# Expert stage: each next weight part is queued behind the instructions that take the same product's result out of PSUM

## The chip, the cores and the metric

The kernel runs on one core of one Trainium2 chip. The metric is the device time of one execution in microseconds (us). A change of less than 0.5% counts here as no change.

## What is computed (reference, cut)

Two layers of a network on 1024 tokens of width 1024, in float32. The first block and the mixer, attention and cross-attention of the second are not touched by the change. What is touched is the last step, a mixture of 32 experts: every token goes to 2 of them, and their weighted results are added to the token's row.

```python
def hierarchical_moe(h, w_group, b_group, w_router, b_router, w_gate_up, w_down):
    ...                                   # two experts e per token, with weights
    def expert_block(args):
        xb, e = args
        gu = xb @ w_gate_up[e]            # 1024 -> 2 x 512
        return (jax.nn.silu(gu[:, :EXPERT_FF]) * gu[:, EXPERT_FF:]) @ w_down[e]   # 512 -> 1024
    ...
    out = jnp.zeros((n + 1, d), ys.dtype).at[buf_tok].add(ys * buf_w[:, None].astype(ys.dtype))
```

## The kernel before, in words

The kernel is one program of which the expert stage (`moe`) is the last part. Up to 96 tokens of an expert are one block; the loop runs over 32 experts.

**Weights.** An expert has 6 MB of weights. They come by SP's queue in transfers of 1 MB into tiles `raw` (line 2187), of which there are 15 (`NRA`, `NRB`, `NRX`, `NRP` = 6, 6, 1, 2); a transfer into a tile is issued when the tile's last reader is done. Each `raw` holds two *parts*. `parts` makes two tiles of a part: ACT copies it into `wh`, rounded (line 154, called through `act` in `split`), and DVE writes what is left over, `raw - wh`, into `wl` (line 166). There are `NP` = 4 buffers of each. So the split of a part waits for its `raw`, for the product of four parts before to have been finished by PE (it frees the buffer), and DVE's half for ACT's.

**Products.** A part feeds one *product*: six matmuls of 512 columns on PE (lines 173 to 175, `mm3`), which add into a PSUM tile. `work` lists the products in order. In the turn of expert e there are eight `up` products of e, namely four into `pg` of c = 0 (the gate) and four into `pg` of c = 1, and then four `down` products of expert e - 1, two into `pd` of c = 0 and two into `pd` of c = 1. Twelve products and six transfers make a turn. `pg` has three PSUM buffers, `pd` two, and `pt` (for transposes) three.

**What takes results out of PSUM.** These instructions run on ACT and DVE too, between the splits:

- `gated` after the last product of a `pg`: for c = 0 a tanh on ACT into `tg` and a product on DVE; for c = 1 a product on DVE.
- `scaled` after the last product of a `pd`: ACT writes half of `y` (line 154). It frees the `pd` buffer. After both halves POOL issues the scatter of `y` (line 2290).
- `x_split` after the sixth product of a turn: PE has transposed the next expert's tokens (line 2232) into `pt`, and ACT and DVE write `xh` and `xl`, in two pieces each.
- `a_split` after the second product of a turn: PE has transposed `tg` of the expert before (line 2263), and ACT and DVE write `ah` and `al`, the left-hand side of its `down` products.

**Order.** Each engine runs its instructions in a fixed order, which a scheduler writes when the program is built. It works with priorities and with estimated times; `tc.issue_after(i)` adds an edge without a semaphore: what is traced under it and runs on the engine of i stands behind i in that engine's order. In the main loop, the results' readers of product n have an edge to the split of part n + 3. The call `ahead(n + NP)`, which traces the split of part n + 4, has none. That split and the readers of product n become possible at the same moment, when PE is through with product n.

Of the kernel before, what the change touches and what calls it, by code (L numbers as in the profile page):

```python
# [16 lines left out]
AF = mybir.ActivationFunctionType  # L17
OP = mybir.AluOpType
# [13 lines left out]
NP = 4  # L32
# [97 lines left out]
class Model:  # L130
# [2077 lines left out]
    def moe(self):  # L2208
        nc, A, tc = self.nc, self.A, self.tc
        with self.pool("moe") as T, self.pool("mg", bufs=3, space=PSUM) as PG, \  # L2210
# [3 lines left out]
            def gather(u):  # L2214
                return nc.gpsimd.indirect_dma_start(
                    out=u["xt"], out_offset=None, in_=self.x3d,
                    in_offset=bass.IndirectOffsetOnAxis(ap=u["row"], axis=0),
                    bounds_check=1023, oob_is_err=False)

            def parts(raw, h):  # L2220

                hi = self.PARTS.tile([128, 2, 512], F32R, name="wh", tag="wh", bufs=NP)
                lo = self.PARTS.tile([128, 2, 512], F32R, name="wl", tag="wl", bufs=NP)
                return (hi, lo, *self.split(hi, lo, raw[:, 2 * h:2 * h + 2]))

            def x_turn(u):
                u["px"] = []
                for q in range(2):
                    pt = PT.tile([128, 4, BLK], F32, name="pt", tag="pt")
                    for a in range(4):  # L2230
                        k = 4 * q + a
                        nc.tensor.transpose(pt[:, a], u["xt"][:, k * 128:(k + 1) * 128], self.ident[0:BLK, 0:BLK])
                    u["px"].append(pt)

            def x_split(u):
                u["xh"] = T.tile([128, 8, BLK], F32R, name="xh", tag="xh", bufs=2)
                u["xl"] = T.tile([128, 8, BLK], F32R, name="xl", tag="xl", bufs=2)
                for q in range(2):
                    self.split(u["xh"][:, 4 * q:4 * q + 4], u["xl"][:, 4 * q:4 * q + 4], u["px"][q])

            def up(u, c, k2, ws):

# [8 lines left out]
            def gated(u, c):  # L2251

                if c == 0:
                    u["t"] = T.tile([BLK, 512], F32, name="tg", tag="tg", bufs=2)
                    self.act(u["t"], u["pg", 0], AF.Tanh, scale=u["half"])
                    self.stt(u["t"], u["t"], 1.0, u["pg", 0], OP.add, OP.mult)
                else:
                    self.tt(u["t"], u["t"], u["pg", 1], OP.mult)

            def a_turn(u):  # L2260
                u["pa"] = PT.tile([128, 4, BLK], F32, name="pt", tag="pt")
                for a in range(4):
                    nc.tensor.transpose(u["pa"][:, a], u["t"][:, a * 128:(a + 1) * 128], self.ident[0:BLK, 0:BLK])

            def a_split(u):
                if u is U[31]:

                    a = T.tile([128, 2, 4, BLK], F32R, name="ahl", tag="xh", bufs=2)
                    u["ah"], u["al"] = a[:, 0], a[:, 1]
                else:  # L2270
                    u["ah"] = T.tile([128, 4, BLK], F32R, name="ah", tag="ah", bufs=1)
                    u["al"] = T.tile([128, 4, BLK], F32R, name="al", tag="al", bufs=1)
                self.split(u["ah"], u["al"], u["pa"])

            def down(u, c, k2, ws):
                if k2 == 0:
# [7 lines left out]
            def scaled(u, c):  # L2284
                if c == 0:
                    u["y"] = T.tile([BLK, 1024], F32, name="y", tag="y", bufs=NY)
                self.act(u["y"][:, c * 512:c * 512 + 512], u["pd", c], AF.Copy, scale=u["gate"])

            def scatter(u):
                return nc.gpsimd.indirect_dma_start(  # L2290
                    out=self.out, out_offset=bass.IndirectOffsetOnAxis(ap=u["row"], axis=0),
                    in_=u["y"], in_offset=None, bounds_check=1023, oob_is_err=False, compute_op=OP.add)

            U = [{"row": self.lsti[:, e:e + 1], "gate": self.lst[:, 1, e:e + 1], "half": self.lst[:, 2, e:e + 1],
                  "xt": xg[e % 3]} for e in range(32)]
# [3 lines left out]
            def beyond():  # L2299


                ov = T.tile([NOV, 5, 32], F32, name="ov", tag="y", bufs=NY)
                one = T.tile([NOV, 128], F32, name="one")
                r, d = T.tile([NOV, 6], F32, name="ovr"), T.tile([NOV, 2, NOV], F32, name="ovd")
                cn = self.cnt[0:NOV]
                nc.vector.memset(one, 1.0)
                nc.vector.tensor_copy(out=r[:, 0:2], in_=self.iop)
                self.ts(ov[:, 0], cn, float(BLK), OP.is_gt)
                for b in range(2, NB):
                    self.stt(ov[:, 0], cn, float(BLK * b), ov[:, 0], OP.is_gt, OP.add)  # L2310
                nc.vector.tensor_tensor_scan(out=ov[:, 1], data0=one[:, 0:32], data1=ov[:, 0], initial=0.0,
                                             op0=OP.mult, op1=OP.add)
                self.tt(ov[:, 2], ov[:, 1], ov[:, 0], OP.subtract)
                self.ts(ov[:, 3], ov[:, 2], r[:, 0:1], OP.is_le)
                self.stt(ov[:, 3], ov[:, 1], r[:, 0:1], ov[:, 3], OP.is_gt, OP.mult)
                self.tt(ov[:, 4], self.io32[0:NOV], ov[:, 3], OP.mult)
                nc.vector.tensor_reduce(out=r[:, 2:3], in_=ov[:, 4], op=OP.add, axis=AX.X)
                self.stt(ov[:, 4], ov[:, 2], r[:, 1:2], ov[:, 3], OP.subtract, OP.mult)
                nc.vector.tensor_reduce(out=r[:, 3:4], in_=ov[:, 4], op=OP.add, axis=AX.X)
                self.stt(r[:, 4:5], r[:, 3:4], -32.0 * BLK, r[:, 2:3], OP.mult, OP.add)  # L2320
                self.ts(d[:, 0], self.ident[0:NOV, 0:NOV], r[:, 4:5], OP.mult)
                self.ts(d[:, 1], self.ident[0:NOV, 0:NOV], r[:, 2:3], OP.mult)
                nc.vector.tensor_copy(out=res[:, 1, 0:1], in_=ov[0:1, 1, 31:32])
                return one, d

            def spread(one, d):
                po = PT.tile([128, 2, NOV], F32, name="po", tag="pt")
                nc.tensor.matmul(po, one, d, start=True, stop=True)
                nc.vector.tensor_copy(out=off, in_=po[:, 0])
                nc.vector.tensor_copy(out=res[:, 0], in_=po[0:1, 1])  # L2330
# [14 lines left out]
            def ahead(n):  # L2345
                if n < len(work):
                    if n % 2 == 0:
                        self.moe_ahead()
                        raws.append(self.moe_raw.pop(0))
                    ready.append(parts(raws[-1], n % 2))  # L2350
# [6 lines left out]
            for n, (f, e, c, k) in enumerate(work):  # L2357
                u = U[e]
                m = f(u, c, k, ready[n][0:2])
                last = ready[min(n + NP, len(work)) - 1]  # L2360
                with tc.issue_after(m.ins):
                    if f is up and (c, k) == (0, 1) and e > 0:
                        a_turn(U[e - 1])
                    if f is up and (c, k) == (1, 1) and e < 31:
                        x_turn(U[e + 1])
                with tc.issue_after(last[2].ins), tc.issue_after(last[3].ins):
                    if f is up and (c, k) == (0, 1) and e > 0:
                        a_split(U[e - 1])
                    if f is up and k == 3:
                        gated(u, c)  # L2370
                    if f is up and (c, k) == (1, 1) and e < 31:
                        x_split(U[e + 1])
                    if f is down and k == 1:
                        scaled(u, c)
                if f is up and (e, c, k) == (31, 1, 3):
                    a_turn(u)
                    a_split(u)
                ahead(n + NP)
                if f is up and (c, k) == (1, 1) and e < 28:
                    with tc.issue_after(put.ins) if e > 1 else nullcontext():  # L2380
                        gather(U[e + 4])
                if f is down and (c, k) == (1, 1):
                    put = scatter(u)
                    if e == OVAT - 1:
                        over = beyond()
                    if e == OVAT + 2:
                        spread(*over)
# [5 lines left out]
            with tc.For_i(0, n_over, 1) as it:  # L2393
# [15 lines left out]
                u = {"row": row, "gate": lst[:, 1:2], "half": lst[:, 2:3], "xt": xg[0]}  # L2409
# [144 lines left out]
```

## Time and profile before

| what | value |
|---|---|
| three runs | 2479.79, 2487.82, 2490.89 us (median 2487.82) |
| the profiled execution | 2485.62 us, of which the span from first to last instruction is 2483.9 us |
| granted TensorE clock, mean over the span | 0.983 |
| PE (matmuls) | 2355.6 us busy, 95% of the span |
| DVE | 1748.2 us, 70% |
| ACT | 1314.5 us, 53% |
| POOL | 341.5 us, 14% |
| DMA, mean over the span | 159 GB/s |

Busy shares are means over stages of unlike kinds. The expert stage takes the last 590 us or so of the span, from 1883 us on. There the DMA engines move some 370 GB/s, and DVE and ACT are far busier than the means above. The ends of matmuls in the trace are modelled, so PE looks busy up to the next matmul even where it is not at its peak; distances between starts are the safer measure.

### The profile page before, as it was taken

To read this page: it belongs to the slowest core of one execution; us is meant where nothing else is said; L and a number is where in the kernel's file an instruction comes from. 1 tells how busy PE (TensorE), PEld (TensorE's weight loads), DVE (VectorE), ACT (ScalarE), POOL (GpSimd) and SP (SyncE) were. 2 spreads that over 40 slices of the span, in tenths; PEclk is the share of its full clock that TensorE was granted. 3 is DMA by queue.
4 is the path that set the end of the run, shared out by engine and by line. 5 is a ranking of instruction groups with operands and counts; after the bars stand their busy time and mean duration, and the time that the engine had idled before them with its cause. 6 is when DMAs were issued, how large, how long until landed. Compare 5 with 4: busy or idle time off the path is not lost. (4 is left out here: it accounts for less than half of the span.)

```text
span 2483.9 us, 35045 instructions
## 1 busy us (share of the span) xinstructions
PE 2355.6 (95%) x13016; PEld 1936.7 (78%) x13016; DVE 1748.2 (70%) x3344; ACT 1314.5 (53%) x2102; POOL 341.5 (14%) x363
## 2 busy tenths in 40 slices
PE   8999989999999999999899899999997999999998
PEld 6888868787888898798798678887885777666765
DVE  9667767677875666666666744235667999898987
ACT  5344532445645455454445432134435888787886
POOL 1011114100021021121121100000011111111111
PEclk9999999999999999999999999999998999999999
DMA  6322353322221111110111456532267999999992
GB/s 222 99 68 67 117 179 127 123 78 84 72 77 39 64 45 42 51 52 35 56 51 40 144 199 221 176 119 77 85 244 271 368 376 373 371 372 359 368 371 66
DMA packets 103838, 394.32 MB, mean 159 GB/s; under 512 B 14129, under 2 KB 33073, under 8 KB 79089
## 3 DMA queue, kind: packets, MB, share of 16 engines
q1 hardware_dynamic: 85008, 335.18, 37.5%
q0 software_dynamic: 18656, 56.88, 7.3%
q8 instruction: 104, 1.70, 0.3%
q14 instruction: 70, 0.57, 0.1%
HBM read 339.07 MB, written 61.31 MB: 161 GB/s over the span
## 5 line engine op out<-in xcount | busy, mean ns | idle before, releaser
L166 DVE TENSOR_TENSOR wl<-raw,wh 128x1024 fp32r<-128x1024 f32 (+1 forms) x496 | 587.7, 1209 | 130.3 <-ACT wh L154 126.1
L154 ACT ACTIVATE wh<-raw 128x1024 fp32r<-128x1024 f32 (+1 forms) x496 | 512.1, 1048 | 250.0 <-PE pj L174 67.2
L173 PE MATMUL pj<-wh,xnh 128*128 128x256 f32 x768 | 222.2, 289 | 2.1 <-ACT tg L154 1.0
L175 PE MATMUL pj<-wh,xnl 128*128 128x256 f32 x768 | 217.2, 283 | 0.0
L174 PE MATMUL pj<-wl,xnh 128*128 128x256 f32 x768 | 217.0, 283 | 0.0
L175 PE MATMUL pg<-wh,xl 128*96 128x512 f32 x512 | 201.3, 393 | 1.6 <-DVE xl L166 1.6
L174 PE MATMUL pg<-wl,xh 128*96 128x512 f32 x512 | 202.6, 396 | 0.0
L173 PE MATMUL pg<-wh,xh 128*96 128x512 f32 x512 | 200.2, 400 | 0.9 <-ACT xh L154 0.9
L173 PEld LDWEIGHTS pj<-wh,xnh 128*128 128x128 f32 x768 | 145.4, 189 | 3.8 <-ACT pc L154 2.5
L174 PEld LDWEIGHTS pj<-wl,xnh 128*128 128x128 f32 x768 | 145.2, 189 | 0.0
L175 PEld LDWEIGHTS pj<-wh,xnl 128*128 128x128 f32 x768 | 145.1, 189 | 0.0
L154 ACT ACTIVATE e<-sc,st,ss 128x1024 f32<-128x1024 f32 (+7 forms) x128 | 105.7, 829 | 54.2 <-DVE st L158 42.4
L178 POOL TENSOR_TENSOR ss<-ss,mhalf 128x4 f32<-128x4 f32 (+1 forms) x68 | 72.7, 1069 | 343.5 <-DVE ss L163 318.4
L173 PE MATMUL pd<-wh,ah 128*96 128x512 f32 x248 | 98.2, 400 | 16.6 <-ACT y L154 16.6
L175 PEld LDWEIGHTS pg<-wh,xl 128*96 128x96 f32 x512 | 83.1, 162 | 38.6 <-DVE xl L166 3.2
L173 PEld LDWEIGHTS pg<-wh,xh 128*96 128x96 f32 x512 | 83.0, 162 | 33.8 <-ACT xh L154 1.3
L174 PEld LDWEIGHTS pg<-wl,xh 128*96 128x96 f32 x512 | 82.8, 162 | 32.4
L173 PE MATMUL pg<-xnh,wh 128*128 128x512 f32 x256 | 104.9, 410 | 0.4 <-ACT kv L154 0.2
L175 PE MATMUL pg<-xnh,wl 128*128 128x512 f32 x256 | 102.6, 401 | 0.0
L173 PE MATMUL pj<-xnh,wh 128*128 128x512 f32 x256 | 102.2, 400 | 0.0
L174 PE MATMUL pg<-xnl,wh 128*128 128x512 f32 x256 | 102.2, 399 | 0.0
L174 PE MATMUL pj<-xnl,wh 128*128 128x512 f32 x256 | 101.2, 396 | 0.0
(998 smaller groups left out, 6327.5 us busy)
## 6 DMA issues: line engine op xcount, KB each, us to landing
raw<-in_w_gu SPq DMA_DIRECT2D x128, 1024.0 KB, 15.3
raw<-in_w_dn SPq DMA_DIRECT2D x64, 1024.0 KB, 15.9
raw<-in_w_out SPq DMA_DIRECT2D x16, 512.0 KB, 4.6
ta<-tg POOLq DMA_DIRECT2D x32, 256.0 KB, 2.5
t<-ta SPq DMA_DIRECT2D x14, 512.0 KB, 3.9
raw<-in_w_ga SPq DMA_DIRECT2D x12, 512.0 KB, 3.7
raw<-in_w_v SPq DMA_DIRECT2D x12, 512.0 KB, 3.5
xraw<-in_xT SPq DMA_DIRECT2D x8, 512.0 KB, 5.8
```

Source lines behind the costliest of these rows:

```text
L154: return self.nc.scalar.activation(out=out, in_=in_, func=func, **kw)
L166: return (eng or self.nc.vector).tensor_tensor(out=out, in0=a, in1=b, op=op)
L173: mm(ps, l[0], r[0], start=start, stop=False)
L174: mm(ps, l[0], r[1], start=False, stop=False)
L175: return mm(ps, l[1], r[0], start=False, stop=stop)
L178: self.nc.gpsimd.tensor_tensor(out=out, in0=in_, in1=self.mhalf[:, :w], op=OP.pow)
```

## The change

The functions that take results out of PSUM now return the instructions they made. The main loop collects them in `out`, and `ahead(n + NP)` is called under an `issue_after` of each. So the ACT half and the DVE half of the split of part n + 4 stand behind those readers of product n that run on the same engine. No instruction is added or taken away, no semaphore and no buffer is changed, and SP's and POOL's queues keep their order, since the edges tie only instructions of one engine.

```diff
@@ x_split
-                for q in range(2):
-                    self.split(u["xh"][:, 4 * q:4 * q + 4], u["xl"][:, 4 * q:4 * q + 4], u["px"][q])
+                return [i for q in range(2)
+                        for i in self.split(u["xh"][:, 4 * q:4 * q + 4], u["xl"][:, 4 * q:4 * q + 4], u["px"][q])]
@@ gated
-                    self.act(u["t"], u["pg", 0], AF.Tanh, scale=u["half"])
-                    self.stt(u["t"], u["t"], 1.0, u["pg", 0], OP.add, OP.mult)
-                else:
-                    self.tt(u["t"], u["t"], u["pg", 1], OP.mult)
+                    return [self.act(u["t"], u["pg", 0], AF.Tanh, scale=u["half"]),
+                            self.stt(u["t"], u["t"], 1.0, u["pg", 0], OP.add, OP.mult)]
+                return [self.tt(u["t"], u["t"], u["pg", 1], OP.mult)]
@@ a_split
-                self.split(u["ah"], u["al"], u["pa"])
+                return self.split(u["ah"], u["al"], u["pa"])
@@ scaled
-                self.act(u["y"][:, c * 512:c * 512 + 512], u["pd", c], AF.Copy, scale=u["gate"])
+                return self.act(u["y"][:, c * 512:c * 512 + 512], u["pd", c], AF.Copy, scale=u["gate"])
@@ main loop
+                out = []
                 with tc.issue_after(last[2].ins), tc.issue_after(last[3].ins):
                     if f is up and (c, k) == (0, 1) and e > 0:
-                        a_split(U[e - 1])
+                        out += a_split(U[e - 1])
                     if f is up and k == 3:
-                        gated(u, c)
+                        out += gated(u, c)
                     if f is up and (c, k) == (1, 1) and e < 31:
-                        x_split(U[e + 1])
+                        out += x_split(U[e + 1])
                     if f is down and k == 1:
-                        scaled(u, c)
+                        out += [scaled(u, c)]
                 ...
-                ahead(n + NP)
+
+                with ExitStack() as es:
+                    for i in out:
+                        es.enter_context(tc.issue_after(i.ins))
+                    ahead(n + NP)
```

What that does to the order is seen on ACT and DVE. Numbers behind a tile's name tell one buffer's use from the next.

ACT, in the second half of the stage, before the change: from the tanh of one expert (`tg`) on, with the two halves of `y` of the expert before.

```order
L154 ACTIVATE tg_20893<-pg_20843,lst_16019 96x512
L154 ACTIVATE wh_20896<-raw_20471 128x1024
L154 ACTIVATE wh_20909<-raw_20502 128x1024
L154 ACTIVATE wh_20935<-raw_20502 128x1024
L154 ACTIVATE wh_20950<-raw_20533 128x1024
L154 ACTIVATE wh_20961<-raw_20533 128x1024
L154 ACTIVATE y_20810<-pd_20791,lst_16019 96x512
L154 ACTIVATE y_20810<-pd_20816,lst_16019 96x512
L154 ACTIVATE wh_20974<-raw_20559 128x1024
```

ACT, the same two halves of `y` and the same tanh after the change.

```order
L154 ACTIVATE wh_20800<-raw_20381 128x1024
L154 ACTIVATE y_20810<-pd_20791,lst_16019 96x512
L154 ACTIVATE wh_20812<-raw_20381 128x1024
L154 ACTIVATE wh_20825<-raw_20422 128x1024
L154 ACTIVATE y_20810<-pd_20816,lst_16019 96x512
L154 ACTIVATE wh_20836<-raw_20422 128x1024
L154 ACTIVATE wh_20852<-raw_20446 128x1024
L154 ACTIVATE ah_20867<-pt_20862 128x384
L154 ACTIVATE wh_20871<-raw_20446 128x1024
L154 ACTIVATE wh_20883<-raw_20471 128x1024
L154 ACTIVATE tg_20893<-pg_20843,lst_16019 96x512
```

Both halves have moved from behind the tanh of the next turn, and behind five splits of that turn, to their own products: eleven splits (from `wh_20812` to `wh_20961`) now stand behind the first half instead of ahead of it. In the first eight full turns `y` stood in these places before the change too.

DVE in one of those first turns, the change against before: the two pieces of `xl` and one split.

```order
 L166 TENSOR_TENSOR wl_18777<-raw_18242,wh_18776 128x1024
 L166 TENSOR_TENSOR wl_18790<-raw_18297,wh_18789 128x1024
-L166 TENSOR_TENSOR wl_18816<-raw_18297,wh_18815 128x1024
 L166 TENSOR_TENSOR xl_18810<-pt_18799,xh_18809 128x384
 L166 TENSOR_TENSOR xl_18810<-pt_18804,xh_18809 128x384
+L166 TENSOR_TENSOR wl_18816<-raw_18297,wh_18815 128x1024
 L166 TENSOR_TENSOR wl_18831<-raw_18426,wh_18830 128x1024
```

One split has changed places with the `xl` pair, and on ACT its `wh` with the `xh` pair. In the same way one split stands behind `ah` and `al` now, where it stood ahead of them. After the change every turn from the second tanh of the stage to the last but one has the same order on ACT: tanh, two splits, two `xh`, four splits, half of `y`, two splits, half of `y`, two splits, `ah`, two splits.

## Rows read from the trace of the kernel before

**Rows 1.** Busy us of each engine (instructions), PEclk, DMA share, GB/s, by stretch.

```profile
1934.52:2075.64 141.12, 141.12 (x673) 100.62 (x672) 133.81 (x159) 121.54 (x145) 26.07 (x17) 1.00 1.02 375
2111.44:2451.89 340.45, 321.40 (x1514) 225.54 (x1513) 303.78 (x307) 277.32 (x326) 46.36 (x34) 1.00 0.95 346
```

**Rows 2.** Timeline of PE: four transposes of `tg`, in four turns (start, us).

```profile
1934.52 0.49 PE L2263 MATMUL pt<-ident,tg 96*128 96x96 f32 x4
...
2075.64 0.49 PE L2263 MATMUL pt<-ident,tg 96*128 96x96 f32 x4
...
2111.44 0.49 PE L2263 MATMUL pt<-ident,tg 96*128 96x96 f32 x4
...
2451.89 0.49 PE L2263 MATMUL pt<-ident,tg 96*128 96x96 f32 x4
```

**Rows 3.** Groups of PE between 2111.6 and 2452 us: the transposes of `tg`.

```profile
L2263 PE MATMUL pt<-ident,tg 96*128 96x96 f32 x74 | 9.2, 245 | 0.0
```

**Rows 4.** Waits, 2111.6 to 2452 us (us in total, times, longest).

```profile
PE pd L173 <- ACT y L154: 16.6, 12, 1.7
...
ACT wh L154 <- DMA raw<-in_w_gu: 0.6, 2, 0.3
```

**Rows 5.** Timeline of ACT and PE at the first of these waits.

```profile
2118.91 1.06 ACT L154 ACTIVATE wh<-raw 128x1024 fp32r<-128x1024 f32 x1 [0.33 <-PE pg L175]
2120.29 1.06 ACT L154 ACTIVATE wh<-raw 128x1024 fp32r<-128x1024 f32 x1 [0.32 <-PE pg L175]
2121.26 1.25 ACT L154 ACTIVATE y<-pd,lst 96x512 f32<-96x512 f32 x2
...
2121.98 0.48 PE L173 MATMUL pd<-wh,ah 128*96 128x512 f32 x1 [1.72 <-ACT y L154]
```

**Rows 6.** Timeline of ACT in an earlier turn, around `y`.

```profile
2088.68 0.69 ACT L154 ACTIVATE y<-pd,lst 96x512 f32<-96x512 f32 x1 [0.55 <-PE pd L175]
2089.27 2.00 ACT L154 ACTIVATE wh<-raw 128x1024 fp32r<-128x1024 f32 x2
2091.45 0.69 ACT L154 ACTIVATE y<-pd,lst 96x512 f32<-96x512 f32 x1 [0.19 <-PE pd L175]
```

**Rows 7.** Waits, 1934.7 to 2075.9 us: DVE for ACT.

```profile
DVE wl L166 <- ACT wh L154: 7.9, 20, 0.6
```

**Rows 8.** Timeline around `x_split` of an early turn: ACT, DVE, then PE.

```profile
2098.88 2.07 ACT L154 ACTIVATE wh<-raw 128x1024 fp32r<-128x1024 f32 x2
2100.85 0.85 ACT L154 ACTIVATE xh<-pt 128x384 fp32r<-128x384 f32 x2
...
2099.00 3.50 DVE L166 TENSOR_TENSOR wl<-raw,wh 128x1024 fp32r<-128x1024 f32 x3 [0.20 <-ACT wh L154]
2102.42 1.01 DVE L166 TENSOR_TENSOR xl<-pt,xh 128x384 fp32r<-128x384 f32 x2
...
2104.74 0.39 PE L174 MATMUL pd<-wl,ah 128*96 128x512 f32 x1
```

**Rows 9.** Timeline around `a_split` of an early turn: ACT, DVE, then PE.

```profile
2111.64 1.06 ACT L154 ACTIVATE wh<-raw 128x1024 fp32r<-128x1024 f32 x1 [0.32 <-PE pg L175]
2112.61 0.47 ACT L154 ACTIVATE ah<-pt 128x384 fp32r<-128x384 f32 x1
...
2112.73 1.23 DVE L166 TENSOR_TENSOR wl<-raw,wh 128x1024 fp32r<-128x1024 f32 x1 [0.16 <-ACT wh L154]
...
2116.17 0.39 PE L174 MATMUL pg<-wl,xh 128*96 128x512 f32 x1
```

**Rows 10.** DMA between 1930 and 2110 us: packets, MB, share.

```profile
q1 hardware_dynamic: 8454, 61.59, 88.9%
```

**Rows 11.** DMA between 2140 and 2410 us.

```profile
q1 hardware_dynamic: 12525, 91.22, 88.7%
```

**Rows 12.** Issues between 1925 and 1940 us: KB each, median us to landing.

```profile
raw<-in_w_gu SPq DMA_DIRECT2D x3, 1024.0 KB, 10.3
```

**Rows 13.** Issues between 2085 and 2100 us.

```profile
raw<-in_w_gu SPq DMA_DIRECT2D x2, 1024.0 KB, 21.4
```

## The prediction

> **What bounds the kernel now.** I read the busy time by stretch first. From 1934 to 2076 us PE is busy for all of 141.12 us, at a granted clock of 1.00; from 2111 to 2452 us it is busy for 321.40 of 340.45 us at the same clock, though the work of a turn is the same [rows 1]. DVE comes close behind (133.81 of 141.12 us), and the DMA engines are fully busy in the early stretch (share 1.02, 375 GB/s). So in the early stretch PE sets the pace, and later something makes PE wait.
>
> How much is lost I read from distances between starts, since matmul ends are modelled. The transposes of `tg` come once a turn. From 1934.52 to 2075.64 us are 8 turns: 141.12 / 8 = 17.64 us a turn [rows 2]. From 2111.44 to 2451.89 us, 340.45 us, the groups of PE hold 74 transposes: two are the end of the first group, whose start is ahead of the window, and 72 are 18 groups of four, so 18 turns [rows 2, 3]. At the early pace 18 turns are 317.52 us. The loss is **22.93 us**.
>
> Then the waits. PE's own wait in that stretch is for `y`, 16.6 us in 12 waits [rows 4]; in the early stretch the busy time leaves no room for one [rows 1]. One wait from near by shows what it is. ACT makes a `wh` at 2118.91 and one at 2120.29 us, each after a wait for PE, and only then both halves of `y`; 0.72 us after they start, PE's first `down` matmul goes, which had waited 1.72 us [rows 5]. So `y` is not long, it is late in ACT's queue: it frees one of two `pd` buffers, and stands behind a split that waits for the product just before the one that needs the buffer. PE must finish that product, ACT see it (0.32 us), split (about 1 us) and write half of `y` (0.7 us): about 2 us in which PE has nothing. In an early turn the halves of `y` stand alone, 2.8 us apart, each soon after its product [rows 6], and nothing waits for them.
>
> **The change, part by part.**
>
> *`y` moved up* (`scaled`). In the order after the change, both halves have the early turns' places in every turn. The 12 waits go. I price this at the whole 22.93 us and not at 16.6: the loss by turns also holds the matmuls that start slowly after a wait, and the short waits for `xh` and `xl` in turns whose order is upset. The lower bound is 16.6 us, the named wait alone [rows 4].
>
> *Two moved pairs.* In all turns, one split now stands behind the `xh`, `xl` pair, and one behind `ah`, `al`. This is new in the early turns too, so the trace shows no such order; I bound it.
>
> - `x_split`: the split ahead of `xh` was the last of ACT's two up to 2100.95 and of DVE's three up to 2102.50 us [rows 8]. Left where it was, `xh` starts at 2100.85 and ends at 2101.70; with the split behind it, `wh` ends by about 2102.7 (1.06 us), and `wl` by 2103.95 (1.22 us). DVE does the `xl` pair (1.01 us) in between, so only the order is changed there. The `wl` is first used by the second matmul of its product, four products on, at 2104.74 [rows 8]. To spare: 0.8 us.
> - `a_split`: `ah` needs the transposes, which start at 2111.44 and take 0.49 us [rows 2]; with ACT's wait for PE (0.3 us) it starts at 2112.2 and ends near 2112.7. The split's `wh` starts there instead of at 2111.64, 1.0 us later, and its `wl` ends at 2112.73 + 1.0 + 1.23 = 2114.96. It is used at 2116.17 [rows 9]. To spare: 1.2 us.
>
> Both are costed at nothing, covered by the three products that PE still has in hand. If the cover is gone, the price is what ACT puts ahead: 0.85 + 0.47 = 1.32 us a turn [rows 8, 9]. Idle time of DVE limits this as well: 141.12 - 133.81 over 8 turns is 0.91 us a turn [rows 1], most of it already waits for `wh`, 7.9 us [rows 7].
>
> *tanh and its product*: already ahead of their split in the early turns; nothing.
>
> *Instructions, buffers, semaphores*: none added. SP's and POOL's queues have the same order, but SP's transfers go out as DVE frees `raw`, so a faster stage asks for weights sooner.
>
> **What is late next: the weights.** A turn at 17.64 us uses six transfers, one every 2.94 us. The hardware queue moved 61.59 MB in 180 us, 342 GB/s [rows 10]: 1.049 MB every 3.06 us; later 91.22 MB in 270 us, 338 GB/s, 3.10 us [rows 11]. So PE at full pace uses weights faster than they come, by 0.12 us a transfer, and lives on what was loaded ahead. Fifteen buffers are 15 x 2.94 = 44.1 us; less 3.6 us between ACT's first read and DVE's last of a tile (2098.88 to 2102.50 [rows 8]), a transfer has 40.5 us from issue to use. At 2085 us it takes 21.4 [rows 13], so 19 us are in reserve. It is used at about 2129, a turn after 2111.44; 17 more turns of six and some five in the last, shorter one make 107 transfers behind it: 107 x 0.12 = 13 us, and 6 us stay. By the landings the reserve melts faster: from 10.3 us at 1930 [rows 12] to 21.4, 11 us over 160 / 2.94 = 54 transfers, 0.20 each, so 107 x 0.20 = 21 us, and the last ten transfers or so are 2 us late. With 338 GB/s in place of 342 as well, 107 x 0.24 = 26 us, 7 us late. I take nothing lost and keep 0 to 7 us. So far ACT waited 0.6 us for weights [rows 4].
>
> The Trainium skill, *DMA: Bandwidth & Descriptors*, section Specifications, speaks against the change here: it puts HBM's share for a core at about 358 GB/s. This trace has 375 [rows 1], so the measurement decides. Were 358 the limit, a transfer would take an estimated 3.06 x 375 / 358 = 3.21 us, the reserve would be short by 107 x 0.27 - 19 = 10 us, and the time 2475 us.
>
> **Sum.** The profiled execution took 2485.62 us (span 2483.9 and 1.7 around it). Less 22.9 it is 2462.7. It lies 2.2 us under the median of the runs, so on the median: 2487.8 - 22.9 = 2464.9, **2465 us**, or 0.92% less.
>
> **Rivals.**
>
> - *The weights become the bound.* For: PE's demand is above the supply, DMA share 1.02. Against: 19 us of reserve, and the gathers end four experts before the end, which leaves the queue more. Gain 22.9 - 7 = 16, so 2472 us; with the lower bound for `y` as well, 16.6 - 7 = 10 and 2478. The page named above has the same mechanism with a lower limit.
> - *The stall only moves* (the change doesn't do what it says for the time): `y` comes early, but the next thing in the upset turns, `xl`, `xh` or `wl`, holds PE as long. For: DVE is busy 95% of an early turn. Against: with the early turns' order all through, those turns show no wait of PE at all. Time 2488 us.
> - *Slower: the two moved pairs outrun their cover.* DVE idles 0.91 us a turn; if the 1.32 us fall on DVE's path whole, each of about 30 turns grows by up to 1.32: +39.6 - 22.9 = +17 us, 2505 us. It decides from 22.9 / 30 = 0.76 us a turn. Against it: 0.8 and 1.2 us to spare above, and three products between a split and its use.
>
> **How the numbers follow.** Forecast 0.73, weights 0.14, stall moves 0.07, slower 0.06. The three runs of before lie up to 8 us under the median and 3 over it, 0.45% from end to end, so about 0.5% (12.4 us) is what can be told from no change. Faster by more than that: under 2475.4 us; the forecast, and most of the weights' case, with something off for the runs' spread: 0.85. Within: the rest of that, and the stall that moves: 0.10. Slower: 0.05. The range goes from 2456 (the fastest run of before, 2479.8, less 22.9, rounded down) to 2478: both lower bounds at once, the weights' 7 us and the 16.6 us, which takes in either alone (2472 and 2471) with the runs' spread. The last two cases are outside.
>
> **What would show it.** Right: in the profile after, the transposes of `tg` come every 17.64 us from about 1934 to the end of the stage; no wait of PE for `y`; PE busy for all of the later stretch; halves of `y` apart on ACT. The group that starts at 2451.89 us [rows 2] comes near 2429. Weights: ACT's waits for `raw` of several us, after 2380 us or so. Slower: PE waiting for `wl` in every turn, and turns over 18.4 us, early ones too. I would be wrong if some instruction that now comes earlier makes DVE wait for ACT more than its 0.9 us a turn.

## The result, and the profile after

| | before | after |
|---|---|---|
| median (lowest to highest), us | 2488.24 (2479.79 to 2490.89), 4 runs | 2463.65 (2462.76 to 2465.11), 4 runs |
| profiled execution (its span), us | 2485.62 (2483.9) | 2462.98 (2460.8) |
| first `pg` matmul to start of the last matmul, us | 1883.38 to 2472.76: 589.38 | 1882.80 to 2450.25: 567.44 |

The ratio is 0.9908, with a 95% interval of 0.9883 to 0.9932: about 0.9% faster, 2463.65 us where 2465 was forecast. The profiled execution is 22.64 us shorter, and 21.94 of that lie in the stage with the experts.

Busy time of the same two stretches after the change, in the columns of [rows 1]; the second reaches over the same 18 turns.

```profile
1934.52:2075.64 141.12, 140.40 (x667) 99.81 (x666) 133.38 (x158) 120.11 (x144) 28.29 (x16) 1.00 1.01 374
2111.86:2429.38 317.52, 317.52 (x1514) 226.46 (x1513) 296.52 (x307) 271.75 (x325) 49.93 (x34) 1.00 1.00 367
```

PE is busy for all of the later stretch, where it was busy for 321.40 of 340.45 us. The two ends of that stretch on PE's timeline, which answer to [rows 2]:

```profile
2111.86 0.49 PE L2262 MATMUL pt<-ident,tg 96*128 96x96 f32 x4
...
2429.38 0.49 PE L2262 MATMUL pt<-ident,tg 96*128 96x96 f32 x4
```

317.52 us for 18 turns are 17.64 us a turn, to the hundredth the pace of the early turns of before. These turns took 340.45 us, so they give 22.93 us. The other sign is in turn 9 of the stage, below: +0.97 us. Together that is 21.96 us, within 0.02 us of the stage's difference.

All waits of PE after the change from 1900 to 2445 us (total, times, longest), where [rows 4] had 16.6 us for `y`:

```profile
PE pg L174 <- DVE wl L166: 0.7, 1, 0.7
PE pd L173 <- ACT ahl L154: 0.2, 1, 0.2
```

ACT at a turn in the part that was slow before, which answers to [rows 5] and reads like [rows 6]:

```profile
2115.39 0.69 ACT L154 ACTIVATE tg<-pg,lst 96x512 f32<-96x512 f32 x1 [0.56 <-PE pg L175]
...
2118.28 0.87 ACT L154 ACTIVATE xh<-pt 128x384 fp32r<-128x384 f32 x2 [0.30 <-PE pt L2232]
...
2124.38 0.69 ACT L154 ACTIVATE y<-pd,lst 96x512 f32<-96x512 f32 x1 [0.55 <-PE pd L175]
2124.96 2.00 ACT L154 ACTIVATE wh<-raw 128x1024 fp32r<-128x1024 f32 x2
2127.15 0.69 ACT L154 ACTIVATE y<-pd,lst 96x512 f32<-96x512 f32 x1 [0.19 <-PE pd L175]
```

The halves of `y` stand apart, 2.8 us from each other, each after a wait of ACT for its own product (0.55 and 0.19 us), and no longer behind the next tanh.

**What is new, and was not foreseen: turn 9.** It takes 18.61 us (17.64 before). PE waits 0.72 us for a `wl`, because DVE has small operations of `beyond()` (a function of the kernel that runs once; tiles `ov`, `ovr`, `ovd`) in one block just ahead of its splits. DVE and PE after the change:

```profile
2053.91 0.17 DVE L166 TENSOR_TENSOR ov<-ov 22x32 f32<-22x32 f32 x1
...
2055.77 0.23 DVE L162 TENSOR_SCALAR ovd<-ident,ovr 22x22 f32<-22x22 f32 x1
2055.91 2.34 DVE L166 TENSOR_TENSOR wl<-raw,wh 128x1024 fp32r<-128x1024 f32 x2
...
2055.83 0.39 PE L175 MATMUL pg<-wh,xl 128*96 128x512 f32 x1
2056.06 0.40 PE L173 MATMUL pg<-wh,xh 128*96 128x512 f32 x1
2057.18 0.48 PE L174 MATMUL pg<-wl,xh 128*96 128x512 f32 x1 [0.72 <-DVE wl L166]
2057.49 0.40 PE L175 MATMUL pg<-wh,xl 128*96 128x512 f32 x1
```

From 2053.91 to 2055.91, 2.0 us, DVE makes no split. Before the change small operations stood between splits (one at 2051.98, the next at 2054.36 us, and two splits between them), and PE did not wait:

```profile
2051.98 0.17 DVE L158 SCALAR_TENSOR_TENSOR ov<-cnt,ov 22x32 f32<-22x32 f32 x1
2052.09 2.34 DVE L166 TENSOR_TENSOR wl<-raw,wh 128x1024 fp32r<-128x1024 f32 x2
2054.36 0.20 DVE L2311 TENSOR_TENSOR_SCAN ov<-one,ov 22x32 f32<-22x32 f32 x1
```

**The weights.** No wait of ACT for `raw` shows from 2111.6 to 2430 us. But transfers take longer from issue to landing. Queue and issues after the change (2140 to 2410 us; then the one transfer issued at 2349.17 us, and the one issued at 2359.03 us; the last number is the median time to landing):

```profile
q1 hardware_dynamic: 12584, 91.64, 88.7%
raw<-in_w_gu SPq DMA_DIRECT2D x58, 1024.0 KB, 25.0
...
raw<-in_w_gu SPq DMA_DIRECT2D x1, 1024.0 KB, 25.9
...
raw<-in_w_dn SPq DMA_DIRECT2D x1, 1024.0 KB, 25.3
```

and before, from 2140 to 2410 us:

```profile
raw<-in_w_gu SPq DMA_DIRECT2D x58, 1024.0 KB, 16.7
```

The queue carries as much as before (91.64 MB in 270 us, [rows 11]: 91.22), yet the median transfer is issued 25.0 instead of 16.7 us ahead of its landing. The reserve, from a transfer's landing to its first reader on ACT, has melted. The first of the tight places is the transfer of 25.9 us, on the timelines of SP's queue and of ACT:

```profile
2349.17 0.33 SPq L2187 DMA_DIRECT2D raw<-in_w_gu  x1
...
2374.69 1.99 ACT L154 ACTIVATE wh<-raw 128x1024 fp32r<-128x1024 f32 x2
```

Issued at 2349.17, it lands 25.9 us later, at 2375.1; the second of the two splits, which begins at about 2375.6, reads it. **0.6 us** of the reserve are left. The tightest comes three transfers later: issued at 2359.03, landed 25.3 us later, at 2384.3, and read at about 2384.6, which leaves 0.3 us. In the same way the reserve is 30.7 us for the tile used at 1962.5 and 20.6 us at 2128.7.

### The profile page after: what moved, and what is told of

The parts are those of the page before. It is cut to its first block, busy times and chain, and to the rows that moved or that the text cites. A ratio compares the mean times of both kernels' runs of the same rounds, so it can differ in the third digit from the quotient of the medians.

```text
span 2460.8 us, 35005 instructions
## 1 busy us (share of the span) xinstructions
PE 2350.5 (96%) x13016; PEld 1934.6 (79%) x13016; DVE 1741.0 (71%) x3344; ACT 1307.3 (53%) x2102; POOL 351.5 (14%) x363
## 5 line engine op out<-in xcount | busy, mean ns | idle before, releaser
L154 ACT ACTIVATE wh<-raw 128x1024 fp32r<-128x1024 f32 (+1 forms) x496 | 503.5, 1044 | 198.1 <-PE pj L174 68.3
L175 PE MATMUL pj<-xnh,wl 128*128 128x512 f32 x256 | 101.3, 396 | 0.0
```

Source lines behind the costliest of these rows:

```text
L154: return self.nc.scalar.activation(out=out, in_=in_, func=func, **kw)
L175: return mm(ps, l[1], r[0], start=False, stop=stop)
```

## Experiments

Each kernel was run beside the kernel before on the same chip, whose median was 2488 to 2491 us throughout; ratios are against that, with 95% intervals. "18 turns" is always the distance that is 317.52 us after the change and 340.45 us before.

**1. Only `y` is tied.** The main loop of the change, where the other three results are no longer collected:

```diff
-                        out += a_split(U[e - 1])
+                        a_split(U[e - 1])
-                        out += gated(u, c)
+                        gated(u, c)
-                        out += x_split(U[e + 1])
+                        x_split(U[e + 1])
                     if f is down and k == 1:
                         out += [scaled(u, c)]
```

> Only the two halves of y are tied: the split of part n + 4 has an edge behind scaled alone; x_split, a_split and gated are left as in the kernel before. The order on ACT is then that of the early turns of before all through (tanh, three splits, two xh, three splits, half of y, two splits, half of y, three splits, ah, split). Theory (the place of y is the whole cause): as fast as the change, 2463.7 us, or up to 1 us faster, since the wait of 0.72 us that the changed kernel has at 2057 us, for a wl, goes. Rival (the moved xh and ah pairs carry part of the gain): between 2468 and 2485 us.

Measured: 2469.27 us (2464.09 to 2472.8), ratio 0.9909 [0.9893, 0.9925]. PE's timeline:

```profile
2121.63 0.49 PE L2262 MATMUL pt<-ident,tg 96*128 96x96 f32 x4
...
2439.15 0.49 PE L2262 MATMUL pt<-ident,tg 96*128 96x96 f32 x4
```

Again 317.52 us. All of the gain is `y`'s. The time is 1.9 us above the change's on the same chip (2467.39 us, experiment 10), and one turn makes most of that: turn 9, with 20.16 instead of 18.61 us, where the expectation had said that its wait would go. ACT's timeline there:

```profile
2064.02 0.68 ACT L154 ACTIVATE y<-pd,lst 96x512 f32<-96x512 f32 x1 [4.01 <-DVE ovr L2318]
```

The first half of `y` waits for an operation of `beyond()` on DVE; in the kernel `ov` takes one of the three buffers of `y`. The `wh` behind it is late by that, and PE waits 1.25 us for it and then 0.78 us for a `wl`.

**2. All but `y` are tied.**

```diff
                     if f is down and k == 1:
-                        out += [scaled(u, c)]
+                        scaled(u, c)
```

> All edges of the change but those of scaled. In the order on ACT the halves of y then stand in the late turns behind the tanh and two splits of the next turn, and on PE the transposes of the next tokens come behind the first down product, while xh stands ahead of the split of the next but one product. Theory (the place of y): y behind two splits costs nothing by itself, since in the turns of before with one to three splits ahead of y PE has no wait; so there is no wait of PE for y. But a split that is tied behind xh must now wait for late transposes; by the early turns' rows PE would miss its wh by some 2 us a turn in about 17 turns, so 2463.7 + 17 x 2 to 3 = 2498 to 2515 us, with waits of PE for wh. Rival (the edges on the pairs carry the gain): 2465 to 2480 us.

Measured: 2514.93 us (2511.35 to 2519.23), ratio 1.0094 [1.0076, 1.0111]: slower than before, at the upper end of what was expected. The waits of PE in the stage:

```profile
PE pd L173 <- ACT wh L154: 29.3, 32, 1.6
```

and ACT's timeline in one turn:

```profile
2185.14 1.24 ACT L154 ACTIVATE y<-pd,lst 96x512 f32<-96x512 f32 x2
2186.28 1.05 ACT L154 ACTIVATE wh<-raw 128x1024 fp32r<-128x1024 f32 x1
2188.10 0.87 ACT L154 ACTIVATE xh<-pt 128x384 fp32r<-128x384 f32 x2 [0.77 <-PE pt L2232]
2188.86 6.03 ACT L154 ACTIVATE wh<-raw 128x1024 fp32r<-128x1024 f32 x6
```

`y` still stands in a pair, ahead of `xh`. PE waits not for it but for the `wh` of the `down` products, which now stand behind `xh`; and `xh` waits for late transposes, 4.5 us behind the start of the tanh (2183.60 us) where it is 2.9 us after the change. The 18 turns take 365.86 us, 48.3 more than after the change, of which 29.3 are this wait of PE. So the other ties give nothing by themselves, and this set of them, without `y`'s, costs.

**3, 4. `y` late in every turn.** Both halves of `y`, and the scatter with them, are put off to the next turn and made to stand there behind the fifth split after the tanh; in the fourth experiment behind the fourth. The splits that follow are tied behind them (`carry`). All other ties of the change stay.

```diff
-                out = []
+                out, carry = carry, []
...
-                    if f is down and k == 1:
+                    if f is down and k == 1 and e > 29:
                         out += [scaled(u, c)]
...
+                if f is up and (c, k) == (1, 3) and e > 1:
+                    with tc.issue_after(ready[-1][2].ins):
+                        carry = [scaled(U[e - 2], 0), scaled(U[e - 2], 1)]
+                    put = scatter(U[e - 2])
```

Experiment 4 has `(c, k) == (1, 2)` in the first of the added lines for `carry`.

> The changed kernel with both halves of y put, by edges on both sides, behind the fifth split after the tanh of the next turn, in 30 turns; the scatter moves with them. Theory (y behind the fifth split makes PE wait for the product before, a split and half of y): each of 30 turns longer by 1.96 us, as the eight such turns of before were, so 2463.7 + 59 = 2522 us, and 30 waits of PE for y of 1.7 us. Rival (those turns were slow for another reason, such as weights that came late or the scheduler's upset order of xh): 2464 to 2480 us.

> The same with the halves of y behind the fourth split, one split earlier. Theory: the turns of before with four splits ahead of y lost 0 (three turns) or had a wait for y of 0.34 us (two turns), so 30 x 0 to 0.5 us: 2464 to 2479 us. Rival (each place that y is later costs alike, so four fifths of 1.96 us a turn): 2463.7 + 30 x 1.57 = 2511 us.

Behind five splits: 2524.6 us (2520.73 to 2528.33), ratio 1.0132 [1.0114, 1.015]; a turn takes 19.6 us. Behind four: 2482.48 us (2479.37 to 2485.28), ratio 0.9968 [0.9954, 0.9982]; 18.2 us a turn. Waits of PE in the stage, of the first:

```profile
PE pd L173 <- ACT y L154: 51.6, 30, 1.7
```

and of the second:

```profile
PE pd L173 <- ACT y L154: 10.2, 30, 0.3
```

One instance of the first, ACT and then PE:

```profile
2149.56 1.06 ACT L154 ACTIVATE wh<-raw 128x1024 fp32r<-128x1024 f32 x1 [0.32 <-PE pg L175]
2150.52 1.24 ACT L154 ACTIVATE y<-pd,lst 96x512 f32<-96x512 f32 x2
2151.24 0.48 PE L173 MATMUL pd<-wh,ah 128*96 128x512 f32 x1 [1.72 <-ACT y L154]
```

This is the stall of [rows 5], 0.32 us, 1.72 us and all, made in 30 turns by `y`'s place alone. Behind five splits `y` costs 1.96 us a turn (19.6 - 17.64), behind four 0.56. So the time does not rise evenly with the place: most of it comes with the fifth split, the one that waits for the product just before `down`. The fourth experiment came out 3.5 us above the range given for it. That range was read from turns of before in which `xh` stands behind `y`; here the two `xh` stand ahead of it, besides the four splits. That this makes the 0.56 us is not shown. (In the kernel before, ten turns have `y` behind five splits: seven took 19.6 us, two 18.94 and one, which also waits for `xh` and `xl`, 21.61.)

**5, 6. Eleven weight buffers for fifteen,** in the kernel after and in the kernel before:

```diff
-NRA, NRB, NRX, NRP = 6, 6, 1, 2
+NRA, NRB, NRX, NRP = 6, 2, 1, 2
```

> The changed kernel with 11 buffers raw in place of 15 (NRB 2 for 6), the same order. In the changed kernel's trace a transfer landed 30.7 us ahead of its first reader at 1962 us and 0.6 us ahead at 2376 us, 140 transfers later: 0.215 us less with each. Four buffers fewer are 4 x 2.94 = 11.8 us less of reserve. Theory (the weights have almost no room left after the change): the reserve is used up some 55 transfers earlier, and from there on every transfer makes the stage 0.2 us later: 10 to 12 us slower than the change, 2474 to 2476 us where the change has 2463.7, with waits of ACT for raw in the last third of the stage. Rival (weights have room to spare, the reserve only looks small because transfers are issued when a buffer is free): no difference, 2464 us.

> The kernel before with 11 buffers raw in place of 15; the order of the late turns stays of the same kind, with 8 turns in which y stands behind five splits. Theory (before the change the waits for y slowed PE enough for the weights to keep some 20 us ahead): 20 - 12 = 8 us stay, so no difference to before, 2486 to 2490 us. Rival (fewer buffers cost time by themselves): about 10 us slower, 2498 us.

With the change: 2476.26 us (2470.66 to 2479.57), ratio 0.9934 [0.9912, 0.9955], at the upper end of what was expected. 18 turns take 326.71 us, 9.2 more; single turns up to 21.18 us, from turn 20 on. ACT's waits in the stage:

```profile
ACT wh L154 <- DMA raw<-in_w_gu: 19.1, 17, 2.9
...
ACT wh L154 <- DMA raw<-in_w_dn: 9.4, 8, 2.2
```

In the kernel before: 2483.25 us (2478.44 to 2488.42), ratio 0.9968 [0.9953, 0.9983], where no difference was expected. The scheduler chose another order in the late turns: 18 turns lose 20.4 instead of 22.9 us, with 14.1 us of waits for `y`. That is 2.5 of the 8 us. Most of the rest goes with the granted TensorE clock: its mean over the span is 0.983 in these ten runs and 0.981 in the seventeen of before beside them, and among those seventeen alone the time falls as it rises, from 2498.4 us at 0.978 to 2480.99 us at 0.985, or some 2 us for each 0.001; by that the difference is worth an estimated 4 to 5 us. In this stage the clock is 1.00, its upper level, in both kernels, so this lies ahead of it; why the clock was higher is open. ACT waits for `raw` for 0.3 us there. So four buffers that the slower kernel doesn't need for its weights are worth 9 us of the change's gain.

**7, 9. A third `pd` buffer,** taken from the `pt` pool: in the kernel of experiment 3, and in the kernel before.

```diff
-                self.pool("md", bufs=2, space=PSUM) as PD, self.pool("mt", bufs=3, space=PSUM) as PT:
+                self.pool("md", bufs=3, space=PSUM) as PD, self.pool("mt", bufs=2, space=PSUM) as PT:
```

> The kernel with both halves of y behind the fifth split in 30 turns (the one expected at 2522 us), with three PSUM buffers for pd and two for pt in place of two and three. Theory (a late y costs because only two pd buffers are there, so that PE's next down product needs the one that y still reads): with a third buffer the first down product has a free one and the second comes two products later, when y is long done; no waits for y, 2464 to 2467 us, as the change. Rival (the place on ACT costs by itself, since y then delays the splits behind it): 2490 to 2522 us.

> The kernel before, without any of the change's edges, with three PSUM buffers for pd and two for pt in place of two and three. The scheduler then writes another order in the late turns: y stands behind up to seven splits, and in several turns xh stands behind it at the end of the turn. Theory (what counts is whether the reader is out of the way before PE needs the buffer or the result; a third buffer moves that point by one product, and the scheduler moves y and xh later still): fewer waits for y, but waits for xh and xl in their place, 2475 to 2492 us. Rival (a third buffer is a cure by itself, as with y behind five splits in every turn): 2464 to 2468 us, as the change.

In the kernel of experiment 3: 2469.51 us (2466.2 to 2471.91), ratio 0.9908 [0.9883, 0.9934]. PE's timeline, and below it all its waits from 1900 to 2460 us:

```profile
2119.13 0.49 PE L2262 MATMUL pt<-ident,tg 96*128 96x96 f32 x4
...
2436.63 0.49 PE L2262 MATMUL pt<-ident,tg 96*128 96x96 f32 x4
```

```profile
PE pd L173 <- ACT ahl L154: 0.4, 1, 0.4
```

`y` is as late as in experiment 3, and costs nothing: 317.50 us. What made it costly is that two buffers leave PE no third to write.

In the kernel before: 2496.48 us (2486.79 to 2501.11), ratio 1.0035 [1.0023, 1.0047], against an expectation of some gain. The same buffers changed the order that the scheduler chose: `y` went behind up to seven splits, and 18 turns took 346.07 us. PE waits there:

```profile
PE pd L173 <- ACT y L154: 9.7, 6, 1.7
PE pg L173 <- ACT xh L154: 5.2, 6, 0.9
PE pg L175 <- DVE xl L166: 4.5, 7, 0.8
```

So a buffer more is a cure only where the order is held; left free, the delay went further and to other tiles.

**8. Two matmuls for three in the experts' products,** on top of the change, to see what bounds next.

```diff
+    def mm2(self, ps, l, r, start, stop):
+        mm = self.nc.tensor.matmul
+        mm(ps, l[0], r[0], start=start, stop=False)
+        return mm(ps, l[0], r[1], start=False, stop=stop)
...
-                    m = self.mm3(u["pg", c], ...
+                    m = self.mm2(u["pg", c], ...
```

> The changed kernel with two of the three matmuls of every piece of a product in the expert stage: the one with xl or al is left out, so PE has a third less to do there; splits and transfers are all made. It measures what stands behind PE now. Theory (weights and DVE are within a few per cent of PE): the weights need some 3.06 us each, 18.4 us a turn once the reserve is gone, and DVE is busy 16.7 of 17.64 us of a turn; so the stage ends with the last transfers and the time is 2450 to 2464 us, though PE has some 160 us less to do. Rival (PE alone bounds the stage): below 2400 us.

One execution, on another chip than the result's: 2459.91 us (span 2457.9). Its busy time from the second tanh's transposes to the last but one, 29 turns:

```profile
1913.85:2424.31 510.46, 418.99 (x1743) 242.71 (x1742) 476.84 (x518) 425.28 (x522) 280.04 (x56) 0.96 1.00 370
```

A third of the products' matmuls is gone, and the mean turn is 510.46 / 29 = 17.60 us. Undisturbed early turns take 16.2 us, and DVE is busy in all of them (81.07 of 81.07 us from 1930.06 to 2011.13 us); later ones take 17 to 20, with ACT waiting for weights:

```profile
ACT wh L154 <- DMA raw<-in_w_gu: 18.8, 15, 2.2
ACT wh L154 <- DMA raw<-in_w_dn: 13.8, 10, 2.4
```

Three turns are much longer. In the turns of 21.85 and 27.54 us ACT waits with the first half of `y`, 6.9 us for an operation of `beyond()` and 13.0 us for a scatter of an earlier `y`: both hold buffers of `y`. In the turn of 25.55 us ACT waits for weights, up to 2.4 us at a time. In all, the 18 late turns take 326.64 us, 9.1 more than after the change, and the turns ahead of them 12.6 less. So with a third less work for PE the span is only 3 us shorter, in one run.

**10. The change once more,** beside the last of these.

> The changed kernel as it is, beside the kernel before on this chip, for the variants above to be compared with: 0.991 of before, 2464 to 2470 us. If the ratio is above 0.9925, the gain of 24.6 us was partly a matter of the first chip.

Measured: 2467.39 us (2466.3 to 2468.82), ratio 0.9919 [0.9904, 0.9934], turn 9 at 18.62 us, the other turns as in the first run of the change. Of the kernels that do all the work none is faster than the change by more than the runs spread.

Here ACT does wait for weights, 2.7 us in five waits, the longest among those for the `down` weights:

```profile
ACT wh L154 <- DMA raw<-in_w_dn: 1.3, 2, 0.9
```

Yet the 18 turns take 317.52 us: a transfer that came up to 0.9 us too late for ACT cost PE nothing there.

## Why the prediction was right

- **The bound and the loss.** PE at 17.64 us a turn was the pace, and 22.93 us were lost in 18 turns. Those turns now take 317.52 us, so the term came out whole. That PE set the pace shows in experiment 8 too: with less work for PE the early turns fall from 17.64 to 16.2 us. The lower bound of 16.6 us was too low by 6.3 us, and both reasons that the prediction gave for taking more are in the trace of before. Its other waits of PE in these turns are 2.5 us:

```profile
PE pg L175 <- DVE xl L166: 1.6, 3, 0.7
PE pg L173 <- ACT xh L154: 0.9, 1, 0.9
```

  The other 3.8 us are 0.24 for each of the 16 waits. Experiment 3 has the same difference (a wait of 1.72 us costs 1.96 a turn), and turn 9 too (0.72 and 0.97). Only part of it is a slow start. In the rows of turn 9 the starts ahead of the wait are 0.23 us apart (2055.83 to 2056.06), but a matmul is modelled as 0.40 us long, so the row counts the wait from 0.17 us too late. The start behind the wait then takes 0.31 us to come (2057.18 to 2057.49), 0.08 more than the 0.23.
- **The mechanism.** A late read of one of two `pd` buffers. Experiment 1 gives the gain by `y` alone, 3 makes the stall in every turn by place alone, and 7 takes it away by a third buffer with the place unchanged. The rival that the stall only moves is out: PE waits 0.9 us in all.
- **The two moved pairs.** Costed at nothing; 18 late turns at 17.64 us in the mean and the early ones at 17.63 to 17.64 say so (one turn between them takes 18.16 us in both kernels). The +0.97 us of turn 9, where the `ov` block takes 2.0 us of DVE and leaves no cover, is not theirs: experiments 2 and 7 tie both pairs, and turn 9 takes 17.64 us there; experiment 1 ties `y` alone, and it takes 20.16. So it comes with `y`'s new place; why the small operations then stand in one block is not shown. The prediction priced turns that looked alike and never looked for work that comes once.
- **The weights.** Nothing was lost, as forecast, but not by the forecast's margin of 6 us, and this part is luck. The reserve at 2128.7 us was 20.6 us (19 predicted). By 2375.6 us, 84 transfers on, 20.0 us were gone, 0.24 a transfer, the highest of the three rates worked out, and not the 0.12 taken. At that rate 107 transfers would have ended 5 us late. What saved it is that the weight queue got faster when the gathers had ended, which the prediction named as an argument and left out of the sum. The last gather is issued at 2365.80 us; from 2340 to 2376 us the weight queue carried 12.31 MB, 342 GB/s, and from 2380 to 2416 us 13.52 MB, 376 GB/s, or 2.79 us a transfer, less than the 2.94 in which PE uses one. The queue of the gathers and scatters went from 0.98 to 0.53 MB, less than the weights gained, so the gathers' bytes are not the whole of it. The reserve then grew to 2 to 5 us. So 0.3 us were left at ACT, and in experiment 10 none, at no cost: a lateness of 0.9 us at ACT was still covered, which the prediction's sum did not count. Experiment 5 shows what the other side looks like.
- **A page that spoke against it.** By the share of HBM that the Trainium skill gives a core (*DMA: Bandwidth & Descriptors*, Specifications) the time would have been 2475 us, an estimate. The two stretches after the change ran at 374 and 367 GB/s over all queues, and the weight queue alone at 376 at the end, so the measurement decides here too. The row there divides the rate of a stack of HBM by two cores, and this program runs on one: it was no limit for this case.

What stays open: why the clock was higher in the runs of experiment 6, the 0.56 us of experiment 4, and why the scheduler lets `y` slip only from the ninth full turn on; the trace shows places, not its reasons.

## What to carry to other kernels

Where a ring of two PSUM buffers is read by an engine that also prepares later work, the read must be issued ahead of any work that waits for the matmuls just before the buffer's next use; behind such work it costs the round trip PE, reader, PE (here 1.96 us a turn behind five splits, the fifth being that work, and 0.56 behind four). Fix the order or add a buffer, but a buffer does not replace an order that is left free, and tying some readers and not the critical one can be worse than tying none. When a stall goes, work out the next resource's reserve by stretches with their own rates: here a 0.9% gain left 0.3 us of 31.

## What the runs showed of the hardware that was not expected

Before, after and in experiment 8 the weight stream ended within 4 us, though PE's last matmuls lie 28 us apart. The last `raw` transfer in these three, then in experiment 3 (windows of its issue, landing time last):

```profile
raw<-in_w_dn SPq DMA_DIRECT2D x1, 1024.0 KB, 12.2
```

```profile
raw<-in_w_dn SPq DMA_DIRECT2D x1, 1024.0 KB, 24.0
```

```profile
raw<-in_w_dn SPq DMA_DIRECT2D x1, 1024.0 KB, 22.4
```

```profile
raw<-in_w_dn SPq DMA_DIRECT2D x1, 1024.0 KB, 7.9
```

Issued at 2424.0, 2415.8 and 2417.1 us, the first three land at 2436.2, 2439.9 and 2439.5. PE's last matmul starts 36.6, 10.4 and 5.6 us behind that (2472.76, 2450.25, 2445.11 us). An earlier issue bought no earlier landing there, only a longer wait in the queue: after the change the time to landing grew from 8.4 us (1925 to 1940 us) to 19.3 (2085 to 2100) and 25.0, while the queue's rate stayed at 339 to 342 GB/s. So the change took away PE's lag behind the stream, and about 10 us are left between the two. It is not so at every speed: in experiment 3, at 19.6 us a turn, the last transfer is issued at 2463.24 us and lands 7.9 us later, at 2471.1; there PE sets when a buffer comes free, and the stream ends later.
